# Attention biases gathered on the host, part tiles of queries and keys written in place, and 58 circulating tiles instead of 66

## The chip, the cores and the metric

The kernel runs on one core of a Trainium2 chip. The metric is the time of one execution on the device in microseconds (us), lower is better. The time before is the median of three runs. A profile of one further execution shows where it goes.

The core has five engines with their own instruction queues: TensorE (PE, the matmuls), VectorE (DVE), ScalarE (ACT), GpSimd (POOL) and SyncE (SP, which in this kernel issues all the DMAs). They wait for one another by semaphores alone.

## The reference

Two layers of a diffusion backbone over 256 latent tokens (a grid of 4 rows of 64) and 256 context tokens, 1024 channels. Each layer is a half-step SwiGLU, a mixer of three branches, and a second half-step SwiGLU. Of the mixer only the two attentions matter here. In the last layer only the latent tokens have queries.

```
u = modulate(rmsnorm(h, g_mix[l]), sh2, sc2)
uc = modulate(rmsnorm(hc, g_mix[l]), csh2, csc2)
nq, nk, nv, fu, wq, wk, wv, gl = split_projection(u @ w_in[l])
...
a = neighbourhood_attention(heads(nq, NA_HEADS), heads(nk, NA_HEADS), heads(nv, NA_HEADS),
                            nk_c, nv_c, na_bias[l], rows)
f = fourier_mix(fu)
w = window_gqa_attention(apply_rope(heads(wq, WA_HEADS), cos, sin),
                         apply_rope(heads(wk, WA_KV_HEADS), cos, sin),
                         heads(wv, WA_KV_HEADS), wk_c, wv_c, wa_sink[l])
h = h + gt2 * merge_branches(a, f, w, gl, w_br[l], w_out[l])
```

Inside the neighbourhood attention (8 heads of 64 channels) the scores of the local keys get a bias that depends on the head and on the distance in rows and columns, and keys outside a window of 16 columns are masked:

```
bias = bias_tab[:, dr_idx[:, None, None, :, None], dc_idx[None, :, :, None, :]]
s_loc = jnp.einsum('brcqhd,brcwkhd->bhrcqwk', qg, kb).astype(jnp.float32) * scale + bias[None]
s_loc = jnp.where(in_win[:, :, None, :], s_loc, NEG_INF)
```

The grid has only 4 rows, so every query sees all rows, and the bias of one head is a table of 256 by 256.

## The kernel before

**Precision.** Everything is float32, done on PE as three matmuls of a reduced type: each operand is split into a high part (a copy by ACT) and a low part (the difference, by DVE, or by POOL for weights in some stages). `mm3` (L286 to L291) issues high by high, high by low and low by high.

**Weights** come as 424 tiles of 512 KB in the order of use: SP loads one (L58), ACT writes the high part (L67), DVE or POOL the low part (L76). Loads run five tiles ahead. Between these, DVE works on the sums of the modulation vectors (L311).

**Tiles.** Activations, parts, scores and all temporary tiles (`act` and `tmp`) come from one pool of `N_ACT` = 66 tiles of 128x512 that circulate: a new tile takes the slot that was freed first, and its writer waits for the last reader of the old one, which can be a DMA.

**The mixer** (`mix`) first runs the fourier branch's first part and the values of the neighbourhood attention, then `attention`, a software pipeline written out in steps g. It goes over blocks of two heads: in layer 0 eight neighbourhood and eight windowed blocks (each four for latent and four for context queries), in layer 1 four and four. In a step: the scores of one group on PE (L726, L727), small parts of an earlier block (DVE, L764), transposes (PE, L757) and their high copy (ACT, L759), the weights of the softmax (DVE L733 with the bias as second operand, ACT L735), the values matmuls (PE, L775). At the end of each step `fill` issues projections on PE by the due times in the table `DUES` (names nk, nq for the neighbourhood half, wk, wq for the windowed one), and runs some pieces of the evacuations that wait in `pending`. Nothing reorders instructions: the order of the code is the order on each engine.

**Evacuation of queries and keys.** A projection's PSUM holds two heads, in partitions 0 to 63 and 64 to 127. `plain` (neighbourhood) or `rope` (windowed, after a rotation with four DMAs at L903 and three POOL instructions at L906) makes a high tile (ACT, L889 or L909) and a low tile (DVE, L891 or L911) over all 128 partitions. Then `stack` (L884) moves halves of them by DMA into the tiles that the scores read: for a query two tiles, each of one head's high and low part in the two halves (4 DMAs); for a key four tiles, each with one head's high or low part in both halves (8 DMAs). There are 26 stacks, 13 in each layer. One DMA moves 64 partitions.

**Bias.** The table in memory is a padded one; `na_bias_load` (L707) reads it with a skewed access pattern, 8 DMAs of 64 KB for each pair of heads, in pieces of 64 elements. Four tiles of the pool for each of two buffers hold it. POOL adds the column mask (L711, four instructions for a pair). Eight tiles are cleared by POOL in their context half at the head of each layer (L444).

Of the kernel before, what the change touches and what calls it, by code (L numbers as in the profile page):

```python
# [7 lines left out]
F32 = mybir.dt.float32  # L8
# [19 lines left out]
BIAS_W = 2 * GRID_W - 1  # L28
# [6 lines left out]
N_ACT = 66  # L35
# [224 lines left out]
class Emit:  # L260
# [102 lines left out]
    def setup(self):  # L363
# [56 lines left out]
        self.na_mask = c.tile([128, NLAT], F32, name="na_mask")  # L420
# [5 lines left out]
    def setup_mix(self):  # L426
# [4 lines left out]
        nc.sync.dma_start(out=self.na_mask, in_=d["na_mask"])  # L431
# [262 lines left out]
    def na_bias_load(self, l, p):  # L694


        nc = self.nc
        tab = self.d["na_bias"]
        for i in range(4):
            t4 = self.nab[p % 2][i][:, :NLAT].rearrange("p (r c) -> p r c", c=GRID_W)  # L700
            hp, qt = divmod(i, 2)
            for r2 in range(2):
                first = WIN_R - 1 - (2 * qt + r2)
                off = ((l * 8 + 2 * p + hp) * GRID_W * (2 * WIN_R - 1) + first) * BIAS_W + GRID_W - 1
                src = bass.AP(tensor=tab.tensor, offset=tab.offset + off,
                              ap=[[(2 * WIN_R - 1) * BIAS_W - 1, GRID_W], [BIAS_W, ROWS], [1, GRID_W]])
                nc.sync.dma_start(out=t4[r2 * 64:r2 * 64 + 64], in_=src)  # L707

    def na_bias(self, p):
        for t in self.nab[p % 2]:  # L710
            self.nc.gpsimd.tensor_tensor(out=t[:, :NLAT], in0=t[:, :NLAT], in1=self.na_mask, op=ALU.add)  # L711
# [132 lines left out]
    def mix(self, l, norm, nxt):  # L844
# [9 lines left out]
        self.na_bias(0)  # L854
        self.na_bias_load(l, 1)
# [374 lines left out]
```

## Time and profile before

| what | us |
|---|---|
| median of three runs | 2122.66 |
| lowest and highest run | 2122.08, 2125.06 |
| the profiled execution | 2120.81 |
| span of its profile | 2119.0 |
| PE busy in the span | 2050.9 |
| DVE busy | 1283.7 |
| ACT busy | 848.5 |
| POOL busy | 355.7 |

The span is the time from the first to the last instruction on the core; the rest of the execution's time lies around it. PE's busy time is modelled from the starts of its pipelined matmuls. A row of a timeline gives a start in the span, a duration, the engine, the line of the kernel and the operation with its output and inputs; "x20" says that so many instructions in a row are drawn together, and the bracket at the end gives the idle time of that engine ahead of it and what ended it.

### The profile page before, as it was taken

How to read it: one execution, taken by the hardware profiler on the slowest of the kernel's cores; microseconds unless marked ns; L12 is line 12 of the kernel's file. 1: busy time of each engine (PE TensorE's matmuls, PEld its weight loads, DVE VectorE, ACT ScalarE, POOL GpSimd, SP SyncE). 2: the span in 40 equal slices, each digit the busy share in tenths (PEclk: the TensorE clock that was granted, in tenths of full speed). 3: DMA queues.
4: the chain of work that ended last, by engine and by line, in shares of the span. 5: the costliest groups of instructions: out<-in, count | busy, mean ns of one | idle time of the engine just before them, and what ended most of it. 6: DMA issues, size and time to landing. Idle time of an engine off the chain costs nothing. (4 is left out here: it accounts for less than half of the span.)

```text
span 2119.0 us, 29168 instructions
## 1 busy us (share of the span) xinstructions
PE 2050.9 (97%) x11193; PEld 1764.7 (83%) x11193; DVE 1283.7 (61%) x2035; ACT 848.5 (40%) x1362; POOL 355.7 (17%) x285
## 2 busy tenths in 40 slices
PE   7899999999999999999999989999999989999998
PEld 3688888878888888988888788888888878999998
DVE  6777776566675334687777465533336548566554
ACT  4422222345786222432222243222324458545443
POOL 4200000403441112300000220000012155330002
PEclk9999999999999999999999999999999999999999
DMA  7465566455532333466666545623344563554663
GB/s 271 139 199 182 196 199 212 124 152 144 136 85 73 100 92 98 150 186 193 199 189 200 186 143 186 199 90 100 99 112 145 145 177 110 160 179 153 186 181 109
DMA packets 119412, 327.05 MB, mean 154 GB/s; under 512 B 30692, under 2 KB 35940, under 8 KB 119272
## 3 DMA queue, kind: packets, MB, share of 16 engines
q1 hardware_dynamic: 119272, 325.18, 50.3%
q8 instruction: 88, 1.44, 0.3%
q14 instruction: 52, 0.43, 0.1%
HBM read 305.99 MB, written 1.05 MB: 145 GB/s over the span
## 5 line engine op out<-in xcount | busy, mean ns | idle before, releaser
L290 PE MATMUL ps<-act,wh 128*128 128x512 f32 (+1 forms) x3227 | 1120.9, 347 | 24.1 <-DVE act L229 13.6
L289 PE MATMUL ps<-act,wh 128*128 128x512 f32 (+1 forms) x3227 | 1121.3, 347 | 3.4 <-ACT act L298 1.9
L291 PE MATMUL ps<-act,wl 128*128 128x512 f32 (+1 forms) x3227 | 1118.9, 347 | 1.8 <-DVE wl L76 1.8
L67 ACT ACTIVATE wh<-raw 128x1024 fp32r<-128x1024 f32 x424 | 447.4, 1056 | 707.8 <-PE ps L290 573.7
L290 PEld LDWEIGHTS ps<-act,wh 128*128 128x128 f32 x3227 | 613.2, 190 | 101.8 <-DVE act L229 14.8
L289 PEld LDWEIGHTS ps<-act,wh 128*128 128x128 f32 x3227 | 613.1, 190 | 78.9 <-ACT act L298 2.5
L291 PEld LDWEIGHTS ps<-act,wl 128*128 128x128 f32 x3227 | 613.1, 190 | 77.9 <-DVE wl L76 2.9
L76 DVE TENSOR_TENSOR wl<-raw,wh 128x1024 fp32r<-128x1024 f32 x379 | 474.6, 1254 | 273.6 <-ACT wh L67 273.0
L311 DVE CUSTOM_DVE_ANT_0 dump<-ada,silu_row 128x1024 bf16<-128x1024 f32 x224 | 273.3, 1220 | 13.9 <-DMA ada<-in_w_ada 11.5
L298 ACT ACTIVATE act<-tmp 128x512 fp32r<-128x512 f32 (+1 forms) x122 | 66.9, 566 | 275.2 <-DVE tmp L516 261.8
L471 DVE SCALAR_TENSOR_TENSOR h<-ps,mod,h 128x256 f32<-128x256 f32 x136 | 61.7, 480 | 150.8 <-PE ps L291 150.8
L76 POOL TENSOR_TENSOR wl<-raw,wh 128x1024 fp32r<-128x1024 f32 x45 | 110.7, 2461 | 222.9 <-ACT wh L67 199.7
L454 POOL TENSOR_TENSOR tmp<-h 128x512 f32<-128x512 f32 (+1 forms) x7 | 11.6, 1661 | 782.3 <-DVE h L471 639.8
L516 DVE TENSOR_TENSOR tmp<-tmp,ps 128x512 f32<-128x512 f32 (+1 forms) x88 | 54.6, 621 | 112.1 <-PE ps L291 107.5
L299 DVE TENSOR_TENSOR act<-tmp,act 128x512 fp32r<-128x512 f32 (+1 forms) x122 | 74.3, 625 | 62.2 <-ACT act L298 62.2
L764 DVE TENSOR_TENSOR act<-ps,act 128x512 fp32r<-128x512 f32 x80 | 54.8, 685 | 35.8 <-ACT act L759 27.6
L735 ACT ACTIVATE tmp<-tmp,sm 128x512 f32<-128x512 f32 (+1 forms) x96 | 62.2, 648 | 32.8 <-DVE sm L733 31.5
L775 PE MATMUL ps<-act 128*128 128x256 f32 x320 | 63.0, 309 | 12.4 <-DVE act L764 11.2
L460 POOL TENSOR_TENSOR tmp<-h 128x256 f32<-128x256 f32 (+1 forms) x44 | 51.7, 1174 | 117.8 <-DVE h L471 112.9
L759 ACT ACTIVATE act<-ps 128x512 fp32r<-128x512 f32 x80 | 47.5, 593 | 39.9 <-PE ps L757 34.5
L444 POOL MEMSET tmp<- 128x256 f32 x16 | 4.8, 312 | 348.6 <-PE ps L291 347.9
L775 PEld LDWEIGHTS ps<-act 128*128 128x128 f32 x320 | 44.8, 189 | 17.5 <-DVE act L764 15.0
(110 smaller groups left out, 1372.8 us busy)
## 6 DMA issues: line engine op xcount, KB each, us to landing
raw<-in_ws SPq DMA_DIRECT2D x424, 512.0 KB, 3.7
ada<-in_w_ada SPq DMA_DIRECT2D x128, 512.0 KB, 3.9
act<-act SPq DMA_DIRECT2D x112, 128.0 KB, 2.3
tmp<-in_w_ada_sc SPq DMA_DIRECT2D x16, 256.0 KB, 5.2
tmp<-in_w_ada SPq DMA_DIRECT2D x16, 256.0 KB, 6.0
tmp<-in_na_bias SPq DMA_DIRECT2D x64, 64.0 KB, 2.7
h<-in_h SPq DMA_DIRECT2D x8, 256.0 KB, 5.2
act<-act SPq DMA_DIRECT2D x32, 64.0 KB, 2.0
```

What stands on the lines that cost most here:

```text
L67: self.nc.scalar.activation(out=wh, in_=self.raw[i], func=AF.Copy)
L76: self.lo_engine.tensor_tensor(out=wl, in0=self.raw.pop(i), in1=self.hi[i].bitcast(F32), op=ALU.subtract)
L289: mm(ps, lhsT=w[0], rhs=x[0], start=start, stop=False)
L290: mm(ps, lhsT=w[0], rhs=x[1], start=False, stop=False)
L291: mm(ps, lhsT=w[1], rhs=x[0], start=False, stop=stop)
L298: nc.scalar.activation(out=hi, in_=src, func=AF.Copy)
L299: nc.vector.tensor_tensor(out=lo, in0=src, in1=hi.bitcast(F32), op=ALU.subtract)
L311: self.nc.vector.tensor_tensor_reduce(out=self.dump[:, ks], in0=w, in1=self.silu_row[:, v, ks], scale=1.0, scalar=m if half else 0.0, op0= ...
L471: self.nc.vector.scalar_tensor_tensor(out=h, in0=ps, scalar=self.mod[l, g][:, v, j:j + 1], in1=h, op0=ALU.mult, op1=ALU.add)
L735: nc.scalar.activation(out=e[:, :nk], in_=e[:, :nk], func=AF.Exp, scale=-1.0, bias=nm, accum_out=b["sum"][:, i:i + 1])
L764: nc.vector.tensor_tensor(out=t[1], in0=ps, in1=t[0].bitcast(F32), op=ALU.subtract)
L775: nc.tensor.matmul(b["ps"][hp][:, :256], lhsT=v, rhs=t[j][:, cs], start=c == 0 and j == 0, stop=c == n - 1 and j == 1)
```

## The change

The change has four parts.

1. **Bias.** The host gathers the biases with the mask into a table of one tile of 128x4x256 for each layer and pair of heads. The kernel loads it with one DMA of 512 KB for each pair. Two fixed tiles of 128x4x512 take the place of eight tiles of the pool. Their context halves are cleared once, at the start of the program, by two POOL instructions instead of sixteen in all. Both first pairs are loaded ahead of the layer's mixer, and pair p + 2 after the weights of block p. POOL's additions of the mask and the mask itself are gone.
2. **Stacks.** `stack` now is the evacuation itself. ACT writes the high part of each head straight into its half of the tile (two instructions of 64 partitions), DVE the low part (two of 64 partitions, into the other half of the same tile for a query). A query needs no DMA, a key four, each of which copies one half of a tile into its other half. The intermediate high and low tiles are gone.
3. The pool has 58 tiles.
4. The host's preparation of the two tables follows.

In counts: bias DMAs 64 to 8, part DMAs 144 to 40, ACT and DVE instructions 26 more each, POOL instructions 46 fewer. The rows of PE are the same in number and order.

```diff
-N_ACT = 66
+N_ACT = 58
...
+        self.nab = [c.tile([128, 4, NT], F32, name=f"nab{i}") for i in range(2)]
+        for t in self.nab:
+            nc.gpsimd.memset(t[:, :, NLAT:], 0.0)
...
-        self.nab = [[self.tmp() for _ in range(4)] for _ in range(2)]
-        for t in self.nab[0] + self.nab[1]:
-            self.nc.gpsimd.memset(t[:, NLAT:], 0.0)
         self.na_bias_load(l, 0)
+        self.na_bias_load(l, 1)
...
+        self.nc.sync.dma_start(out=self.nab[p % 2][:, :, :NLAT], in_=self.d["na_bias"][l, p])
...
-        self.na_bias(0)
-        self.na_bias_load(l, 1)
...
-        def stack(name, hi, lo, n):
-
-
-            a, b = self.act(), self.act()
+        def stack(name, src, scale, n):
+
+
             x, y = slice(0, 64), slice(64, 128)
+            a, b = self.act()[:, :n], self.act()[:, :n]
             if "q" in name[0]:
-                moves = (a, x, hi, x), (a, y, lo, x), (b, x, lo, y), (b, y, hi, y)
-                res[name] = a, b
+                parts = (a, x, a, y, x), (b, y, b, x, y)
+                moves = ()
             else:
-                c, d = self.act(), self.act()
-                moves = ((a, x, hi, x), (a, y, hi, x), (b, x, hi, y), (b, y, hi, y),
-                         (c, x, lo, x), (c, y, lo, x), (d, x, lo, y), (d, y, lo, y))
-                res[name] = a, b, c, d
-            for t, i, s, j in moves:
-                nc.sync.dma_start(out=t[i, :n].bitcast(F32), in_=s[j, :n].bitcast(F32))
+                c, d = self.act()[:, :n], self.act()[:, :n]
+                parts = (a, x, c, x, x), (b, y, d, y, y)
+                moves = (a, x, y), (b, y, x), (c, x, y), (d, y, x)
+            for hi, i, _, _, s in parts:
+                nc.scalar.activation(out=hi[i], in_=src[s], func=AF.Copy, scale=scale)
+            yield
+            for hi, i, lo, j, s in parts:
+                nc.vector.scalar_tensor_tensor(out=lo[j], in0=src[s], scalar=scale, in1=hi[i].bitcast(F32),
+                                               op0=ALU.mult, op1=ALU.subtract)
+            for t, i, j in moves:
+                nc.sync.dma_start(out=t[j].bitcast(F32), in_=t[i].bitcast(F32))
+            res[name] = (a, b) if "q" in name[0] else (a, b, c, d)
...
-        def bias_ahead(p):
-            self.na_bias(p)
-            if p < 3:
-                self.na_bias_load(l, p + 1)
...
-                            after=(lambda: bias_ahead(p + 1)) if lat and p < 3 else None,
-                            mask=self.nab[p % 2] if lat else [zero] * 4,
+                            after=(lambda: self.na_bias_load(l, p + 2)) if lat and p < 2 else None,
+                            mask=[self.nab[p % 2][:, i, :] for i in range(4)] if lat else [zero] * 4,
```

Three places show how the order of instructions changes. The first is SP's queue in layer 1's attention, ahead of and behind the first bias load between two blocks; raw is a weight tile, act with 64x512 or 64x256 a part move. Before:

```order
L884 DMA act_13638<-act_13632 64x512 x2
L58 DMA raw_13667<-in_ws 128x1024
L707 DMA tmp_12402<-in_na_bias 64x4x64 x2
L707 DMA tmp_12403<-in_na_bias 64x4x64 x2
L707 DMA tmp_12404<-in_na_bias 64x4x64 x2
L707 DMA tmp_12405<-in_na_bias 64x4x64 x2
L884 DMA act_13697<-act_13693 64x256
L884 DMA act_13697<-act_13694 64x256
L884 DMA act_13698<-act_13694 64x256
L884 DMA act_13698<-act_13693 64x256
L58 DMA raw_13740<-in_ws 128x1024
```

The same place of SP's queue in the changed kernel:

```order
L870 DMA act_13474<-act_13474 64x512
L57 DMA raw_13503<-in_ws 128x1024
L694 DMA nab0_279<-in_na_bias 128x4x256
L57 DMA raw_13561<-in_ws 128x1024
L870 DMA act_13581<-act_13581 64x512
L870 DMA act_13582<-act_13582 64x512
L870 DMA act_13583<-act_13583 64x512
L870 DMA act_13584<-act_13584 64x512
L57 DMA raw_13633<-in_ws 128x1024
```

The eight bias DMAs became one, the query's four moves between two weight loads are gone, and the next key has four moves instead of eight.

The second is DVE's queue at the stack of the windowed keys in layer 1; L733 (ISA) are the weights, L764 the low part that the values matmuls read. Before:

```order
L733 ISA tmp_14090,sm_13962<-ps_14074,tmp_12405 128x512
L733 ISA sm_13962 128x1
L911 SCALAR_TENSOR_TENSOR act_14104<-tmp_13991,act_14103 128x512
L764 TENSOR_TENSOR act_14087<-ps_14081,act_14086 128x512
L733 ISA tmp_14156,sm_14140<-ps_14144,tmp_12406 128x512
```

In the changed kernel (L716 is the former L733, L867 the former L911, L747 the former L764):

```order
L716 ISA tmp_13892,sm_13764<-ps_13876,nab0_279 128x512
L716 ISA sm_13764 128x1
L867 SCALAR_TENSOR_TENSOR act_13903<-tmp_13793,act_13901 64x512
L867 SCALAR_TENSOR_TENSOR act_13904<-tmp_13793,act_13902 64x512
L747 TENSOR_TENSOR act_13889<-ps_13883,act_13888 128x512
L716 ISA tmp_13950,sm_13934<-ps_13938,nab1_280 128x512
```

One instruction of 128 partitions ahead of the low part became two of 64.

The third is POOL's queue at the start of the program; L76 is a weight's low part, L221 and L229 lead to the first projection's operand. Before:

```order
L454 TENSOR_TENSOR tmp_211<-h0_112 128x512
L76 TENSOR_TENSOR wl_261<-raw_136,wh_259 128x1024
L221 TENSOR_TENSOR tmp_287<-h0_112,tmp_268 128x512
L221 TENSOR_TENSOR tmp_301<-h1_113,tmp_268 128x512
L229 TENSOR_TENSOR act_291<-tmp_288,act_290 128x512
```

In the changed kernel:

```order
L452 TENSOR_TENSOR tmp_211<-h0_112 128x512
L75 TENSOR_TENSOR wl_261<-raw_136,wh_259 128x1024
L421 MEMSET nab0_279 128x4x256
L421 MEMSET nab1_280 128x4x256
L220 TENSOR_TENSOR tmp_290<-h0_112,tmp_268 128x512
L220 TENSOR_TENSOR tmp_304<-h1_113,tmp_268 128x512
L228 TENSOR_TENSOR act_294<-tmp_291,act_293 128x512
```

The two memsets came in between the first low part of a weight and the first L221.

## Rows read from the trace of the kernel before

**Rows 1.** The page's first part: busy us of an engine, its share of the span, and its instructions.

```profile
PE 2050.9 (97%) x11193; PEld 1764.7 (83%) x11193; DVE 1283.7 (61%) x2035; ACT 848.5 (40%) x1362; POOL 355.7 (17%) x285
```

**Rows 2.** The windows: from and to in us, length, then the busy time (and instructions) of PE, PE's weight load, DVE, ACT and POOL, the granted clock of PE as a share of full speed, the DMA share and GB/s.

```profile
500.00:640.00 140.00, 135.16 (x758) 114.47 (x757) 98.30 (x254) 102.95 (x256) 63.11 (x53) 1.00 0.48 124
...
1700.00:1750.00 50.00, 40.12 (x256) 35.55 (x255) 23.17 (x52) 27.30 (x56) 29.13 (x26) 0.97 0.65 164
...
1715.00:1720.00 5.00, 1.67 (x8) 1.47 (x9) 2.70 (x6) 1.90 (x4) 1.23 (x2) 0.85 0.90 303
1720.00:1725.00 5.00, 4.59 (x28) 4.00 (x26) 1.12 (x3) 2.63 (x5) 2.40 (x1) 0.81 0.94 202
```

**Rows 3.** The timeline of PE from 1716 to 1724 us.

```profile
1716.16 0.62 PE L775 MATMUL ps<-act 128*128 128x256 f32 x3 [2.86 <-DVE act L764]
1718.95 1.12 PE L932 MATMUL ps<-ident,tmp 128*128 128x128 f32 x4 [2.17 <-ACT tmp L928]
...
1720.08 0.41 PE L290 MATMUL ps<-act,wh 128*128 128x256 f32 x1
1720.29 0.41 PE L291 MATMUL ps<-act,wl 128*128 128x256 f32 x1
...
1723.25 0.28 PE L289 MATMUL ps<-act,wh 128*128 128x256 f32 x1
1723.37 0.28 PE L290 MATMUL ps<-act,wh 128*128 128x256 f32 x1
```

**Rows 4.** The timeline of SP's queue, 1664 to 1752 us; the second number is the time that SP took to issue them.

```profile
1670.34 17.01 SPq L884 DMA_DIRECT2D act<-act  x20
...
1706.67 7.82 SPq L884 DMA_DIRECT2D act<-act  x12
...
1716.14 5.93 SPq L707 DMA_DIRECT2D tmp<-in_na_bias  x8
```

**Rows 5.** The timeline of DVE, 1705 to 1726 us.

```profile
1707.56 0.42 DVE L891 SCALAR_TENSOR_TENSOR act<-ps,act 128x256 fp32r<-128x256 f32 x1 [7.51 <-DMA act<-act]
...
1715.42 0.69 DVE L764 TENSOR_TENSOR act<-ps,act 128x512 fp32r<-128x512 f32 x1 [7.37 <-DMA act<-act]
```

**Rows 6.** The timeline of PE at three other gaps, one in layer 0 and two in layer 1.

```profile
514.53 0.50 PE L726 MATMUL ps<-act 128*128 128x512 f32 x1 [1.83 <-DMA act<-act]
...
1747.27 0.47 PE L726 MATMUL ps<-act 128*128 128x512 f32 x1 [0.41 <-DMA act<-act]
...
1749.70 0.62 PE L775 MATMUL ps<-act 128*128 128x256 f32 x3 [1.18 <-DVE act L764]
```

**Rows 7.** Groups of instructions by line and form: count, busy us in all, mean ns of one, idle time before them and what ended it.

```profile
L889 ACT ACTIVATE act<-ps 128x512 fp32r<-128x512 f32 x12 | 7.0, 584 | 1.4 <-PE ps L291 1.4
L889 ACT ACTIVATE act<-ps 128x256 fp32r<-128x256 f32 x4 | 1.5, 367 | 0.0
L781 ACT ACTIVATE tmp<-ps 64x256 f32<-64x256 f32 x96 | 36.1, 376 | 2.3 <-PE ps L775 1.2
L911 DVE SCALAR_TENSOR_TENSOR act<-tmp,act 128x512 fp32r<-128x512 f32 x6 | 5.0, 831 | 4.1 <-ACT act L909 4.1
L911 DVE SCALAR_TENSOR_TENSOR act<-tmp,act 128x256 fp32r<-128x256 f32 x4 | 3.8, 946 | 6.1 <-ACT act L909 6.1
...
L76 DVE TENSOR_TENSOR wl<-raw,wh 128x1024 fp32r<-128x1024 f32 x379 | 474.6, 1254 | 273.6 <-ACT wh L67 273.0
```

**Rows 8.** Layer 0's windowed blocks: the timeline of DVE and of PE at one stack, and PE's waits for DVE's low part, in all, their number and the longest, first from 480 to 720 us (layer 0), then from 1730 to 1800 us (layer 1).

```profile
590.54 0.69 DVE L911 SCALAR_TENSOR_TENSOR act<-tmp,act 128x512 fp32r<-128x512 f32 x1 [0.65 <-ACT act L909]
...
591.91 0.63 PE L775 MATMUL ps<-act 128*128 128x256 f32 x3 [0.34 <-DVE act L764]
...
PE ps L775 <- DVE act L764: 2.2, 7, 0.3
...
PE ps L775 <- DVE act L764: 6.2, 6, 1.9
```

**Rows 9.** Layer 1's windowed stacks: the timelines of DVE and POOL.

```profile
1733.73 1.22 DVE L911 SCALAR_TENSOR_TENSOR act<-tmp,act 128x512 fp32r<-128x512 f32 x1 [1.41 <-ACT act L909]
...
1746.39 2.38 POOL L76 TENSOR_TENSOR wl<-raw,wh 128x1024 fp32r<-128x1024 f32 x1
...
1746.92 2.13 DVE L911 SCALAR_TENSOR_TENSOR act<-tmp,act 128x256 fp32r<-128x256 f32 x1 [2.02 <-ACT act L909]
...
1773.46 0.46 DVE L911 SCALAR_TENSOR_TENSOR act<-tmp,act 128x256 fp32r<-128x256 f32 x1 [1.38 <-ACT act L909]
```

**Rows 10.** The head of the mixer in layer 0 and in layer 1: timelines of DVE, POOL and PE.

```profile
417.33 0.82 DVE L214 SCALAR_TENSOR_TENSOR act<-tmp,mod,act 128x256 fp32r<-128x256 f32 x1
...
1615.34 3.55 POOL L711 TENSOR_TENSOR tmp<-tmp,na_mask 128x256 f32<-128x256 f32 x4
...
1618.22 2.88 DVE L76 TENSOR_TENSOR wl<-raw,wh 128x1024 fp32r<-128x1024 f32 x2
...
1620.02 0.50 PE L587 MATMUL ps<-wl,act 128*128 128x512 f32 x1 [2.11 <-DVE wl L76]
...
1627.18 0.48 DVE L214 SCALAR_TENSOR_TENSOR act<-tmp,mod,act 128x256 fp32r<-128x256 f32 x1
```

**Rows 11.** POOL's timeline at the start of the program and at the first eight memsets.

```profile
32.25 1.67 POOL L229 TENSOR_TENSOR act<-tmp,act 128x512 fp32r<-128x512 f32 x1 [2.27 <-ACT tmp L227]
...
232.18 2.80 POOL L444 MEMSET tmp<- 128x256 f32 x8 [158.34 <-PE ps L291]
```

More of the change, by code (lines that the diff above doesn't have):

```diff
@@ L27 @@
 WINDOW = 128
-BIAS_W = 2 * GRID_W - 1
 O_NA_Q, O_NA_K, O_NA_V, O_FN, O_WA_Q, O_WA_K, O_WA_V, O_GATE = (
@@ L430, in setup_mix @@
         nc.sync.dma_start(out=self.sin, in_=d["sin"])
-        nc.sync.dma_start(out=self.na_mask, in_=d["na_mask"])
         nc.sync.dma_start(out=self.wa_mask, in_=d["wa_mask"])
@@ L694, in na_bias_load @@
     def na_bias_load(self, l, p):
[L697 to L711, printed above, removed]
+        self.nc.sync.dma_start(out=self.nab[p % 2][:, :, :NLAT], in_=self.d["na_bias"][l, p])
     def attention(self, makers, fill):
@@ L868, in project @@
                 yield
[L870 to L873 removed]
+        def stack(name, src, scale, n):
             x, y = slice(0, 64), slice(64, 128)
+            a, b = self.act()[:, :n], self.act()[:, :n]
             if "q" in name[0]:
[L876 to L894 removed]
+                parts = (a, x, a, y, x), (b, y, b, x, y)
+                moves = ()
+            else:
+                c, d = self.act()[:, :n], self.act()[:, :n]
[10 more added lines that the diff above has]
+            res[name] = (a, b) if "q" in name[0] else (a, b, c, d)
+        def plain(scale):
+            return lambda name, ps, n: stack(name, ps[:, :n], scale, n)
         def rope(scale):
@@ L907, in evac @@
                 yield 1
-                hi, lo = self.act(), self.act()
-                nc.scalar.activation(out=hi[:, :n], in_=t, func=AF.Copy, scale=scale)
-                yield
-                nc.vector.scalar_tensor_tensor(out=lo[:, :n], in0=t, scalar=scale, in1=hi[:, :n].bitcast(F32),
-                                               op0=ALU.mult, op1=ALU.subtract)
-                stack(name, hi, lo, n)
+                yield from stack(name, t, scale, n)
             return evac
@@ L1137, in constants @@
     cos, sin = np.cos(ang).T, np.sin(ang).T
-    c = np.arange(GRID_W)
-    start = np.clip(c - WIN_C // 2, 0, GRID_W - WIN_C)
-    inside = (c[None] >= start[:, None]) & (c[None] < start[:, None] + WIN_C)
-    na = np.where(inside, 0.0, NEG).astype(f)
     band = np.where(np.abs(t[:, None] - t[None]) <= WINDOW, 0.0, NEG).astype(f).reshape(2, 128, NLAT)
@@ L1154, in constants @@
         "sin": np.concatenate([-sin, sin] * 2, 0),
-        "na_mask": np.tile(na, (2, ROWS)),
         "wa_mask": wa,
@@ L1175, in pack @@
     a["w_ada_sc"] = w["w_ada"][0, :, D:2 * D].reshape(KD, 128, 2, 512).transpose(2, 0, 1, 3)
-    pad = GRID_W - WIN_C
-    t = np.pad(w["na_bias"], ((0, 0), (0, 0), (0, 0), (pad, pad)))
-    a["na_bias"] = np.broadcast_to(t[:, :, None], t.shape[:2] + (GRID_W,) + t.shape[2:])
+    c, t = np.arange(GRID_W), np.arange(NLAT)
+    start = np.clip(c - WIN_C // 2, 0, GRID_W - WIN_C)
+    inside = (c[None] >= start[:, None]) & (c[None] < start[:, None] + WIN_C)
+    row, col = t // GRID_W, t % GRID_W
+    dr = row[None] - row[:, None] + WIN_R - 1
+    dc = np.clip(col[None] - col[:, None], 1 - WIN_C, WIN_C - 1) + WIN_C - 1
+    b = np.full((DEPTH, 8, NLAT, NLAT), NEG, np.float32)
+    inside = np.tile(inside, (ROWS, ROWS))
+    b[:, :, inside] = w["na_bias"][:, :, dr[inside], dc[inside]]
+    a["na_bias"] = b.reshape(DEPTH, 4, 2, 2, 128, NLAT).transpose(0, 1, 4, 2, 3, 5).reshape(DEPTH, 4, 128, 4, NLAT)
     s = w["wa_sink"]
@@ L1209 @@
     "c": (128, KD, 2), "b_ada": (128, DEPTH, 9, KD), "gains": (128, DEPTH, 3, 8), "g_final": (128, 8),
-    "na_bias": (DEPTH, 8, GRID_W, 2 * WIN_R - 1, BIAS_W), "sink": (DEPTH, 4, 4), "ident": (128, 128),
-    "cos": (128, NLAT), "sin": (128, NLAT), "na_mask": (128, NLAT), "wa_mask": (128, 2, NT),
+    "na_bias": (DEPTH, 4, 128, 4, NLAT), "sink": (DEPTH, 4, 4), "ident": (128, 128),
+    "cos": (128, NLAT), "sin": (128, NLAT), "wa_mask": (128, 2, NT),
     "dft_n": (128, 2 * NLAT), "dft_d": (128, 256),
```

9 lines of the change are left out of this document (removed).

## The prediction

> **What bounds the kernel now.** I read the busy shares first [rows 1]: TensorE (PE) is busy for 97% of the span. The order of its instructions is the same in both programs, row for row, so the change can win or lose only what PE waits for, some 68 us in all. Next I read the windows [rows 2], to see which stage holds such waits near the edit. Layer 0's attention, 500 to 640 us, has 4.84 us of idle PE in 140. The stretch 1700 to 1750 us, the head of layer 1's attention, has 9.88 in 50, and 3.33 of these fall into 1715 to 1720 alone. Then I read PE's own timeline there [rows 3]: two gaps, 2.86 us ahead of a values matmul that waits for VectorE's (DVE's) low part, and 2.17 us ahead of a transpose that waits for ScalarE (ACT). Why both engines are late stands in the queue of SyncE (SP) [rows 4] and in their own rows [rows 5]. SP issues part moves and bias pieces back to back from 1670 to 1722 us. The low part of a projection waits 7.51 us and the next low part 7.37 us, both released by a part move. An act slot is free only when the moves that read it have gone, and SP issues one in 0.65 to 0.85 us (7.82 us for 12 moves, 17.01 us for 20). So at this place SP's queue, not an engine, sets the end. It is the one place where the removed work is on the path for long.
>
> **The change, part by part.**
>
> *Term A, the queue in layer 1.* Between 1670 and 1722 us SP issues 48 part moves and 16 bias pieces. In the new order the same stretch has 16 part moves (keys only) and two bias loads. At 0.65 to 0.85 us each that is 12 to 15 us of issuing in 52, so the backlog cannot form. Besides, no slot that a query's parts need is held by a DMA any more. I count both gaps as gone: 2.86 + 2.17 = 5.03 us. The clock goes with them: the granted clock is 0.85 and then 0.81 in the two windows after the gap [rows 2], and matmuls of 256 columns start 0.21 us apart there, against 0.12 after 1723 us [rows 3]. Ten of them, and the scores behind, lose 1.2 us. A = **6.2 us**. What is late next there is the usual chain of a block, ACT's copy and DVE's low part, whose gaps are priced below (term E). A new wait is SP's own: the load of the pair two ahead stands right behind the weights of the block that last read that buffer, so SP waits for DVE there, with weight tiles queued behind. Weights are loaded five tiles ahead, so I price that at nothing; if the cover were gone it would be one wait of up to about 1 us for each of 4 loads.
>
> *Term B, later part moves.* The scores at 1747.27 us wait 0.41 us for a move, and the values matmul at 1749.70 another 1.18 us for a low part that came behind a slowed stack [rows 6]. I take the whole of the first and half of the second: **1.0 us**, between 0.4 and 1.6.
>
> *Term C, layer 0.* One scores matmul at 514.53 us waits 1.83 us for a move [rows 6]. It is a query's or a key's; SP's backlog is gone in either case, but a key still has one move per part where it had two. I take **1.8 us** (at worst half of it).
>
> *Term D, POOL's additions of the mask.* 32 of these go. Most run beside nothing that PE waits for. At the head of each mix four of them run beside DVE's evacuations [rows 10]: in layer 1 a pair of weight subtractions takes 2.88 us, where one takes 1.25 on average [rows 7], and PE waits 2.11 us for it; in layer 0 an L214 beside them takes 0.82 us, one that stands alone 0.48. I count 0.7 for layer 1 and 0.5 for layer 0: **1.2 us** (from 0 to 2).
>
> Gains: 6.2 + 1.0 + 1.8 + 1.2 = 10.2 us.
>
> *Term E, the added halves.* Each of 26 stacks has one more ACT and one more DVE instruction, since each now writes 64 partitions. Half the partitions do not halve the time: ACT's copies of 64x256 take 376 ns, those of 128x256 take 367 [rows 7]. So a 512-column stack adds 0.58 us on ACT [rows 7] and 0.69 on DVE [rows 8], a 256-column one 0.37 [rows 7] and 0.46 [rows 9]. The two overlap: DVE can take the first half while ACT writes the second, so the delay of what stands behind is about one half-instruction, start to start: I use 0.62 us for 512 columns (0.69 less the 0.07 by which rows of one engine overlap) and 0.4 for 256. The 16 stacks of the neighbourhood half lie where DVE and ACT wait more than they work (DVE 98 of 140 us in layer 0 [rows 2]), and PE showed no gap behind them but those above: I take nothing, at most 0.62 each. The five windowed ones in layer 0 are different. There DVE's row stands right ahead of the low part that PE waits for: L911 at 590.54, and PE's gap of 0.34 us ends at 591.91 [rows 8]. A gap there means no slack, so the half adds its full 0.6 us. PE has seven such gaps in layer 0's attention, and I take four of the five stacks to have one: 2.4 us. In layer 1, from 1730 us on, there are six, up to 1.9 us long. The first stack has 512 columns, but today it is slowed to 1.22 us beside POOL's mask additions, which go (one alone takes 0.69), so it comes out even [rows 9]; the other four, of 256 columns, add 0.4 us each, 1.6 us (0 to 1.8). E = **4.0 us**, between 1 and 8.
>
> *Term F, the two memsets at the start.* Sixteen memsets leave a place where POOL is idle, and two of 128x4x256 come in ahead of the first L221, on the way to PE's first projection. By elements they cost what eight did, 2.80 us [rows 11]. POOL is idle for 2.27 us before its L229 at 32.25 (it waits for ACT), which covers all but 2.8 - 2.3 = 0.5 us. L221 slows DVE beside it, and that moves along: I take **0.6 us**, between 0 and the whole 2.8 if the cover is gone.
>
> *Term G, 58 slots in place of 66.* Eight slots went to the two bias tiles, which held eight before; the stacks hold two tiles less while they run. Whether PE's reading of an old tile now holds up a new one no row can tell, since before it never came so close. Below it is 0, above the 2.86 us of the gap that such a wait made in [rows 3]; I take **0.5 us**, near the lower end, because a slot returns as soon as its last reader is done, and that is now an engine a few instructions back instead of a queue of DMAs.
>
> Sum: -10.2 + 4.0 + 0.6 + 0.5 = -5.1 us. On the profiled execution, 2120.81 us (its span is 2119.0), this gives 2115.7. That execution lies 1.85 us under the median of the runs, 2122.66, so for the median I say **2117.6 us**.
>
> **A rule of the skill, as a rival.** Two of the windowed stacks' DVE instructions are far longer beside POOL's work: 1.22 us, and 2.13 beside a subtraction of 2.38 us on POOL that began 0.53 us earlier, against 0.46 alone [rows 9]. Over all ten, 8.8 us against about 6.0 at their undisturbed lengths [rows 7]: 2.8 us of excess. Mechanism: each such instruction reads two SBUF tiles, and stands still until POOL's instruction is done; two halves can be caught twice, if POOL gets its next instruction in between them. Price: once more 2.8 us, all of it ahead of low parts that PE waits for, so -5.1 + 2.8 = -2.3, or 2120.4 us. For it: POOL is busy 63.11 of 140 us in layer 0's attention [rows 2], so a next instruction is often ready. Against it: the halves are issued without a gap, and POOL's row is mostly over when the first begins. The Trainium skill states this as a lock (SBUF — State Buffer, "Who interferes with whom"): a VectorE instruction with two SBUF inputs and a GpSimd instruction that reads SBUF block one another, and the one issued second waits for all of the other. The 2.13 us here agrees with a wait nearly as long as the rest of POOL's 2.38; by that rule the sum would be -2.3.
>
> **Other rivals.** *Slower: the halves cost everywhere.* If ACT and DVE have no slack in the neighbourhood stages either, all 26 stacks come through: 18 x 0.62 + 8 x 0.4 = 14.4 us in place of 4.0. Then the sum is -10.2 + 14.4 + 1.1 = +5.3, or 2128 us. It decides for slower once the halves cost over 13.3 us. For it: ACT's copy and DVE's low part stand in the same chain at every stack. Against it: PE showed gaps of 0.34 us at most behind such rows in layer 0. *No gain: the stall comes back.* The gap in layer 1 may come from too many live tiles, with the DMAs only the last reader in the row; with 58 slots the writer then waits for PE's reads at the same place. A falls from 6.2 to about 1.5 us: -0.4, or 2122.3 us. Against it: the 7.5 us waits are released by moves, which are gone. *More gain: the halves hide.* If E is 1 and D 2, the sum is -11.0 + 1.0 + 1.1 = -8.9: 2113.8 us, and with no cost in F and G 2112.7, down to 2111 if B is 1.6 and a gap of about 1 us behind a windowed stack closes as well.
>
> **How the numbers follow.** My forecast, 2115 to 2120, has a chance of 0.50, the larger gain 0.14, the halves caught by POOL 0.13, the stall that returns 0.13, and the halves everywhere 0.10. A measurement of this kernel can tell a change of about 0.2%, 4.25 us, from none: faster is under 2118.4, slower over 2126.9. The forecast's upper end (0.08), the rival by POOL and the returned stall are within it: same 0.34; slower 0.10; faster 0.56. The range leaves out the halves everywhere and the last of the larger gain: 2111 to 2124.
>
> **What would show it.** In the new profile: SP's rows between 1660 and 1720 us with gaps; no DVE or ACT wait on a part move of several us; PE's gaps at the first layer 1 block gone, with a granted clock of 1.00 there; DVE's halves as pairs of about 0.69 us with PE gaps of 0.6 to 1 us behind those of the windowed stacks; the first L221 some 2.8 us later, and PE's first L229 wait at most 0.6 us longer. I am wrong if PE's gap at 1716 stays under another releaser, or if new gaps of 0.3 to 0.6 us appear behind the neighbourhood stacks of layer 0.

## The result, and the profile after

The changed kernel is slower: 2133.93 us (median of four runs, 2131.18 to 2135.33) against 2122.37 for the kernel before, ratio 1.0053 with a 95% interval of 1.0036 to 1.0071. The forecast was 2117.6, its range 2111 to 2124. The profiled execution has a span of 2132.3 us, 13.3 more than before.

The page's first part of the changed kernel answers to [rows 1]:

```profile
PE 2058.4 (97%) x11193; PEld 1770.6 (83%) x11193; DVE 1311.7 (62%) x2061; ACT 864.5 (41%) x1388; POOL 328.3 (15%) x239
```

PE has the same instructions and is busy for 7.5 us more; it is idle for 73.9 us where it was 68.1, 5.8 more. The two make the 13.3. So over half of the net loss is not idle time at all: matmuls ran longer, at a lower clock. The windows of the changed kernel (columns as in [rows 2]) show where:

```profile
500.00:640.00 140.00, 129.59 (x693) 109.19 (x692) 100.02 (x236) 98.80 (x234) 48.43 (x35) 0.96 0.27 77
580.00:585.00 5.00, 3.39 (x12) 2.61 (x13) 3.07 (x10) 2.61 (x7) 0.00 (x0) 0.77 0.02 6
640.00:700.00 60.00, 57.37 (x305) 47.84 (x304) 38.36 (x85) 45.06 (x106) 16.72 (x13) 1.00 0.25 71
1700.00:1750.00 50.00, 44.54 (x270) 38.86 (x268) 32.52 (x61) 30.29 (x61) 25.69 (x18) 0.97 0.52 146
1750.00:1800.00 50.00, 41.55 (x299) 38.73 (x299) 41.22 (x79) 37.38 (x92) 25.10 (x18) 0.93 0.27 80
1785.00:1790.00 5.00, 3.96 (x17) 3.86 (x18) 4.88 (x9) 2.64 (x6) 2.38 (x1) 0.50 0.16 29
```

PE's idle time in layer 0's attention went from 4.84 to 10.41 us [rows 2], although the gap of 1.83 us at its head [rows 6] is gone. The head of layer 1's attention, 1700 to 1750 us, went from 9.88 to 5.46, much as forecast; the next 50 us have 8.45, where they had 3.14. And behind most of the new gaps the granted clock falls: 0.77 from 580 to 585 us, 0.50 (the lower level, 1.2 of 2.4 GHz) from 1785 to 1790. Fewer matmuls fit into such a stretch, and they count as busy.

Fixed stretches of time hold different work in the two kernels. PE's rows are the same in number and order, so the same matmuls can also be found in both traces by their place in the order. Two stretches of the kernel before, layer 0's windowed blocks and layer 1's attention behind its head:

```profile
560.19:640.01 79.82, 76.81 (x443) 64.94 (x442) 61.55 (x161) 65.08 (x170) 34.98 (x30) 1.00 0.38 101
1725.96:1800.08 74.12, 67.49 (x508) 62.64 (x509) 58.98 (x123) 59.67 (x142) 44.38 (x36) 1.00 0.41 116
```

The same matmuls in the changed kernel:

```profile
559.57:654.21 94.64, 82.61 (x442) 68.83 (x441) 70.50 (x166) 68.97 (x175) 34.91 (x30) 0.95 0.20 58
1731.88:1813.97 82.09, 70.94 (x508) 65.85 (x509) 64.58 (x128) 62.28 (x147) 41.93 (x32) 0.94 0.30 86
```

They take 14.8 us longer in layer 0 (9.0 of idle time, 5.8 of longer matmuls) and 8.0 longer in layer 1 (4.5 and 3.5). That is 22.8 us lost. The profiled execution is only 13.3 longer, so all other stretches together gained about 9.5.

PE's timeline in layer 0's windowed blocks has three new gaps:

```profile
581.61 0.62 PE L758 MATMUL ps<-act 128*128 128x256 f32 x3 [2.32 <-DVE act L747]
...
599.06 0.62 PE L758 MATMUL ps<-act 128*128 128x256 f32 x3 [2.54 <-DVE act L747]
...
623.60 1.01 PE L758 MATMUL ps<-act 128*128 128x256 f32 x3 [2.55 <-DVE act L747]
```

The bracket names the low part that the values matmuls read, as in [rows 8], where the gap behind a stack was 0.34. What made it late stands in the timelines of DVE and POOL. First the kernel before, at the same stack:

```profile
576.98 0.69 DVE L911 SCALAR_TENSOR_TENSOR act<-tmp,act 128x512 fp32r<-128x512 f32 x1 [1.18 <-ACT act L909]
...
577.06 2.84 POOL L76 TENSOR_TENSOR wl<-raw,wh 128x1024 fp32r<-128x1024 f32 x1
```

Then the changed kernel:

```profile
576.98 3.44 DVE L867 SCALAR_TENSOR_TENSOR act<-tmp,act 64x512 fp32r<-64x512 f32 x2 [1.19 <-ACT act L864]
...
577.07 2.81 POOL L75 TENSOR_TENSOR wl<-raw,wh 128x1024 fp32r<-128x1024 f32 x1
...
577.70 2.73 DVE L867 SCALAR_TENSOR_TENSOR act<-tmp,act 64x512 fp32r<-64x512 f32 x1
...
580.88 0.67 DVE L747 TENSOR_TENSOR act<-ps,act 128x512 fp32r<-128x512 f32 x1
```

(The row at 577.70 is the second half by itself; the row at 576.98 has both.) Read them together. In both kernels a weight's low part on POOL begins, by its row, some 0.1 us after DVE's instruction. It takes 2.8 us there instead of the usual 2.4, which I read as a wait for DVE. Before, DVE was then done, and its next low part (L764, with an input in PSUM) did not mind POOL. Now a second half is next. It is issued right behind the first, but POOL's instruction stands ahead of it, and the half takes 2.73 us. The pair takes 3.44 us, to 580.42, 0.5 us past POOL's end at 579.88. Undisturbed, the two would have ended at about 578.4. The low part behind them comes some 2 us late, and PE waits. The second half reads nothing that this instruction of POOL writes, and no semaphore is between them. So engines here do not wait for one another by semaphores alone, and such a wait shows in no bracket, only as a longer instruction.

Of the ten pairs three take 3.44 or 3.45 us, all in layer 0. Four take 0.4 to 1.2 us more than undisturbed, beside shorter instructions of POOL or the end of a longer one, and three lose nothing.

### The profile page after: what moved, and what is told of

The parts are those of the page before. It is cut to its first block, busy times and chain, and to the rows that moved or that the text cites. A ratio compares the mean times of both kernels' runs of the same rounds, so it can differ in the third digit from the quotient of the medians.

```text
span 2132.3 us, 28797 instructions
## 1 busy us (share of the span) xinstructions
PE 2058.4 (97%) x11193; PEld 1770.6 (83%) x11193; DVE 1311.7 (62%) x2061; ACT 864.5 (41%) x1388; POOL 328.3 (15%) x239
## 3 DMA queue, kind: packets, MB, share of 16 engines
HBM read 305.86 MB, written 1.05 MB: 144 GB/s over the span
## 5 line engine op out<-in xcount | busy, mean ns | idle before, releaser
L747 DVE TENSOR_TENSOR act<-ps,act 128x512 fp32r<-128x512 f32 x80 | 55.0, 687 | 25.4 <-ACT act L742 24.5
L735 DVE TENSOR_SCALAR tmp<-tmp,sm 128x512 f32<-128x512 f32 (+1 forms) x96 | 59.1, 657 | 1.1
```

The source lines that it names most:

```text
L735: nc.vector.tensor_scalar(out=e, in0=e, scalar1=b["r"][:, i:i + 1], scalar2=None, op0=ALU.mult)
```

## The experiments

Three theories were set against one another. **1:** between two halves on DVE, each with both inputs in SBUF, POOL gets in with an instruction that reads SBUF, and the second half waits for all of it. **2:** 58 tiles are too few. **3:** the halves cost their own length in the chain, as term E of the prediction had it. All ratios are against the kernel before on the same chip.

### Which stacks

**windowed_whole** takes the ten windowed stacks back to the form of before and leaves the rest of the change:

```diff
-                yield from stack(name, t, scale, n)
+                yield from moved(name, t, scale, n)
```

(`moved` is the old evacuation: one ACT and one DVE instruction of 128 partitions, then `stack`'s old moves.) Expected:

> The changed kernel with its ten windowed stacks (wk, wq) made as before: one ACT and one DVE instruction over 128 partitions, then the moves by DMA; the neighbourhood stacks, the bias and the 58 tiles stay as changed. Theory 1 (between the two halves of a windowed low part a POOL instruction gets in, and the second half waits for all of it): the DVE instructions take 0.5 to 1.3 us each again, PE's idle time in layer 0's windowed blocks falls from 9.8 us (560 to 640) to 3 to 4, the clock stays at 1.00, and the time is 2113 to 2119 us. Theory 2 (58 tiles are too few, and writers wait for readers): each of these stacks needs two more tiles, so the gaps stay or grow: 2133 us or more. Theory 3 (the halves cost their own length everywhere, with POOL or without): 16 of 26 stacks still have halves, so two thirds of the loss stay: about 2129 us.

Measured: 2118.23 us, ratio 0.9981 (0.9972 to 0.9989). Some 16 us of the changed kernel's time went with ten pairs of halves, while 16 stacks still had theirs. That fits theory 1 and not 3. In layer 0 the matmuls counted above take the time of the kernel before again (79.96 us against 79.82), at full clock:

```profile
558.32:638.28 79.96, 76.96 (x442) 64.92 (x441) 61.81 (x161) 65.02 (x170) 35.10 (x30) 1.00 0.38 101
```

In layer 1 they still take 5.6 us longer than before; late tiles have a part in that (below).

**neighb_whole** is the mirror image (`plain` calls `moved`, `rope` the new `stack`). Expected:

> The mirror image: the sixteen neighbourhood stacks (nk, nq) as before, whole and with moves by DMA, the windowed ones in halves as changed. Theory 1: the pairs of windowed halves still take up to 3.4 us beside POOL, the gaps of 2 to 4 us stay, and some of the queue of SP in layer 1 comes back: 2133 to 2140 us. Theory 3: ten of 26 stacks have halves left, so the time is about 2126 us.

Measured: 2140.53 us, ratio 1.0083 (1.0070 to 1.0096). That is 0.5 us past what theory 1 expected. The gaps of 2.3 to 2.6 us are all there, and SP's moves cost some more (a scores matmul in layer 0 waits 4.57 us for one, where it waited 1.83 in the kernel before): theory 1 again, and far from theory 3's 2126.

**before_split** asks the question from the other side: the kernel before, with nothing changed but the windowed low part cut in two.

```diff
-                nc.vector.scalar_tensor_tensor(out=lo[:, :n], in0=t, scalar=scale, in1=hi[:, :n].bitcast(F32),
-                                               op0=ALU.mult, op1=ALU.subtract)
+                for s in slice(0, 64), slice(64, 128):
+                    nc.vector.scalar_tensor_tensor(out=lo[s, :n], in0=t[s], scalar=scale, in1=hi[s, :n].bitcast(F32),
+                                                   op0=ALU.mult, op1=ALU.subtract)
```

> The kernel before with one edit: each of its ten windowed low parts is made by two DVE instructions of 64 partitions instead of one of 128; ACT, the moves, the bias and the 66 tiles are as before. Theory 1 (POOL gets in between two halves): the pairs take up to 3.4 us, PE's gaps in layer 0's windowed blocks grow from 0.34 to over 2 us at three or four stacks, the clock falls behind them, and the time is 2128 to 2136 us. Theory 3 (the halves cost their own length): ten times at most 0.6 us, 2122 to 2128 us. If the loss needs ACT's halves or the 58 tiles as well: 2121 to 2124 us.

Measured: 2147.09 us, ratio 1.0111 (1.0096 to 1.0125), 24 us slower, more than expected and twice the loss of the whole change. Ten additional DVE instructions did that. The timelines of DVE and POOL at one stack, and the group by line and form:

```profile
577.67 3.44 DVE L912 SCALAR_TENSOR_TENSOR act<-tmp,act 64x512 fp32r<-64x512 f32 x2 [1.53 <-ACT act L909]
...
577.75 2.81 POOL L76 TENSOR_TENSOR wl<-raw,wh 128x1024 fp32r<-128x1024 f32 x1
```

```profile
L912 DVE SCALAR_TENSOR_TENSOR act<-tmp,act 64x512 fp32r<-64x512 f32 x12 | 15.6, 1302 | 4.6 <-ACT act L909 4.4
```

Neither ACT's halves nor the tiles are needed for the loss. The matmuls counted above take 16.2 and 8.9 us longer here than in the kernel before, 25.1 of the 26.4 us between the two spans:

```profile
560.23:656.29 96.06, 82.83 (x443) 69.48 (x441) 70.61 (x166) 65.42 (x170) 35.22 (x30) 0.93 0.32 84
1743.50:1826.48 82.98, 70.20 (x508) 65.20 (x509) 63.96 (x128) 59.50 (x142) 45.19 (x36) 0.96 0.37 104
```

The changed kernel loses 22.8 us there. That it is slower by only half as much is due to what it gains elsewhere.

### Is it POOL's reading?

**pool_writes_only** leaves DVE as it is in the changed kernel and takes POOL's reads away. It leaves out the low parts of the weights that POOL makes during attention; they are zeros.

```diff
+            if self.lo_engine is self.nc.gpsimd and self.clear:
+                self.raw.pop(i)
+                self.nc.gpsimd.memset(wl.bitcast(F32), 0.0)
```

> The changed kernel with the low parts of the weights that POOL makes during attention left out: POOL clears those tiles instead (an instruction that writes and reads nothing), so the products with these low parts are missing. DVE and ACT have the same instructions as in the changed kernel. Theory 1 (the second half waits while POOL reads SBUF): pairs of windowed halves of 64x512 fall from 3.4 to about 1.3 us, the PE gaps of 2.3 to 2.6 us in layer 0 to under 1 us, and the time to 2117 to 2124 us. Theory 3 (the halves cost their own length): DVE's work is unchanged, so about 2134 us. A third possible reading, that POOL's mere being busy slows DVE, expects pairs of 1.9 us or so beside a clearing instruction of about 1 us.

Measured: 2115.80 us, ratio 0.9972 (0.9961 to 0.9983). The same pair of halves, beside an instruction of POOL that starts at the same point but only writes (timelines, then the group by line and form):

```profile
576.12 1.40 DVE L872 SCALAR_TENSOR_TENSOR act<-tmp,act 64x512 fp32r<-64x512 f32 x2 [1.19 <-ACT act L869]
...
576.19 0.95 POOL L78 MEMSET wl<- 128x1024 f32 x1
```

```profile
L872 DVE SCALAR_TENSOR_TENSOR act<-tmp,act 64x512 fp32r<-64x512 f32 x12 | 8.6, 721 | 4.2 <-ACT act L869 4.0
```

1.40 us for the pair instead of 3.44, and a mean of 721 ns, where the changed kernel's groups by line and form have 1270; its halves that read PSUM, by contrast, are not slowed, though seven of the 32 run beside a subtraction on POOL:

```profile
L867 DVE SCALAR_TENSOR_TENSOR act<-ps,act 64x512 fp32r<-64x512 f32 x24 | 16.5, 688 | 12.0 <-ACT act L864 11.5
L867 DVE SCALAR_TENSOR_TENSOR act<-tmp,act 64x512 fp32r<-64x512 f32 x12 | 15.2, 1270 | 4.2 <-ACT act L864 4.0
```

The clearing instruction is shorter too (0.95 against 2.4 us), so being short could explain a part; but the pair loses almost nothing, not a wait of 0.9 us. The Trainium skill (SBUF — State Buffer, "Who interferes with whom") says exactly this: a VectorE instruction with two SBUF inputs contends with a GpSimd instruction that reads SBUF, not with one that only writes it, and the later one waits for all of the other. The runs agree: 3.44 us beside the instruction that reads, 1.40 beside the one that only writes, 688 ns a half with an input in PSUM.

The time came out 1.2 us below what theory 1 expected. In layer 0 the matmuls counted above take 3.0 us longer than in the kernel before, not 14.8; that is near the 2.4 us that term E has for this layer. In layer 1 3.4 of the 8.0 us stay:

```profile
558.73:641.54 82.81, 77.49 (x443) 65.07 (x441) 60.24 (x166) 68.49 (x175) 22.90 (x30) 1.00 0.24 66
1719.77:1797.29 77.52, 69.18 (x508) 64.90 (x509) 55.57 (x130) 62.07 (x147) 27.03 (x32) 0.96 0.31 92
```

There POOL's rotation, which this run leaves as it is, reads two tiles, and a pair beside it is as long as in the changed kernel, 1.82 us against 1.40 undisturbed (DVE and POOL):

```profile
1727.70 1.82 DVE L872 SCALAR_TENSOR_TENSOR act<-tmp,act 64x512 fp32r<-64x512 f32 x2 [1.40 <-ACT act L869]
...
1727.76 1.21 POOL L891 TENSOR_TENSOR tmp<-tmp,sin 128x256 f32<-128x256 f32 x1
```

**halves_apart** keeps DVE's halves and POOL's reads and puts a step of the pipeline between the halves:

```diff
             for hi, i, lo, j, s in parts:
+                if late and lo is not parts[0][2]:
+                    yield 1
```

> The changed kernel, but the second half of a windowed low part is issued one step of the pipeline later, so that the low part which the values matmuls read stands between the halves. Theory 1: POOL's instruction still gets in behind the first half, but the values' low part (one operand in PSUM) does not wait for it, so a half meets POOL's instruction only if that one is still running: most gaps of 2.3 us shrink to under 1 us, 2118 to 2126 us. Theory 3: the work is the same and stands in the same chain: about 2134 us.

Measured: 2126.35 us, ratio 1.0019 (1.0010 to 1.0027): half of the loss over windowed_whole stays, and the time is 0.35 us past what theory 1 expected. A mean of 1227 ns for its windowed 64x512 halves says that they still meet POOL; but the low part that PE needs no longer stands behind them.

**low_on_pool** gives the windowed low halves to POOL, so that POOL's own order keeps them from its weights (the scale goes into the first copy):

```diff
+                if name[0][0] == "w":
+                    nc.gpsimd.tensor_tensor(out=lo[j], in0=src[s], in1=hi[i].bitcast(F32), op=ALU.subtract)
```

> The changed kernel with the windowed low halves made by POOL instead of DVE (the scale, a power of two, is put into the first copy, so a subtraction is enough). Then POOL's own order keeps a weight's low part and a half apart, and DVE's instruction ahead of the values' low part is gone. Theory 1: the gaps of 2 to 4 us behind windowed stacks go, 2113 to 2121 us; POOL has some 26 us more to do, and if it becomes late with the weights' low parts PE shows gaps that wait for them. Theory 3: half of the added work, ACT's, stays in the chain: 2122 to 2128 us.

Measured: 2118.53 us, ratio 0.9985 (0.9977 to 0.9994). ACT's halves are still there, DVE's are gone, and the time is that of windowed_whole. PE has no gap of 2 us left in the two attentions, and no lower clock. But it is so in the sum only: in layer 0 the matmuls counted above still take 7.7 us longer than before, in layer 1 none. What POOL's own time for the halves and ACT's halves have in the 7.7 us was not tried.

### The tiles and the bias

**halves_62_tiles** is the changed kernel with 62 tiles. Room for four more comes from keeping the zeros of the context half once in each bias tile:

```diff
-N_ACT = 58
+N_ACT = 62
-        self.nab = [c.tile([128, 4, NT], F32, name=f"nab{i}") for i in range(2)]
+        self.nab = [c.tile([128, 5, NLAT], F32, name=f"nab{i}") for i in range(2)]
...
-                            mask=[self.nab[p % 2][:, i, :] for i in range(4)] if lat else [zero] * 4,
+                            mask=[self.nab[p % 2][:, i::4 - i, :][:, :2] for i in range(4)] if lat else [zero] * 4,
```

> The changed kernel with 62 circulating tiles: the zeros of the bias tiles' context halves are kept once in each bias tile and read by a stepped pattern, which frees the room. Theory 1: DVE's and ACT's waits in the windowed blocks are not for slots, so 2131 to 2136 us. Theory 2 (58 tiles are too few): the waits behind the halves go too, under 2126 us.

Measured: 2134.85 us, ratio 1.0053 (1.0040 to 1.0066), the changed kernel's own. Theory 2 falls for the change as it stands.

It does not fall for the others. **windowed_whole_62**:

> The kernel with whole windowed stacks, and 62 tiles in the same way. With 58 its trace has DVE's low parts in layer 1 released by POOL's rotation (1.42 and 2.40 us) and one DVE instruction by a part move (1.51 us), though neither is an operand of them: slots that come back late. If that is so, these waits go and PE's gaps in layer 1's windowed blocks shrink by 3 to 5 us: 2113 to 2116 us. If the slots are not the cause: 2117 to 2119 us as with 58.

Measured: 2114.95 us, ratio 0.9962 (0.9950 to 0.9975), 3.3 us under the same with 58. The two intervals just touch, so this size is rough. What went are waits like these of windowed_whole, on DVE's and POOL's timelines:

```profile
1728.16 0.69 DVE L747 TENSOR_TENSOR act<-ps,act 128x512 fp32r<-128x512 f32 x1 [1.42 <-POOL tmp L905]
...
1727.41 0.72 POOL L905 TENSOR_TENSOR tmp<-tmp 128x256 f32<-128x256 f32 x1
```

L747 has no operand of POOL's; it waits until POOL has read the tile that was in its slot before (1727.41 + 0.72 = 1728.13).

**bias_only** is the bias part alone, with all stacks as before and 58 tiles, **bias_only_62** the same with 62.

Expected of the first:

> The bias part and the 58 tiles alone: gathered on the host, one load for a pair, no additions on POOL; all 26 stacks whole with moves by DMA as before. Theory 1: no halves, so the windowed gaps are those of before or less; the queue of SP in layer 1 loses 16 of 64 issues and keeps the 48 moves, so the gap of 5 us there shrinks by about a quarter to a half: 2117 to 2122 us. Theory 2: the stacks need their two more tiles from 58: slower than before, 2126 us or more.

and of the second:

> The bias part alone (all 26 stacks whole, with moves by DMA) with 62 tiles instead of the 58 at which it was 3 us slower than before. If slots that come back late were the cause of that: 2117 to 2121 us. If SP's queue, which still has 48 moves to issue in layer 1, is: 2124 to 2127 us, with the gaps at 515 us and at the first block of layer 1 still there.

Measured: 2125.51 us, ratio 1.0011 (1.0002 to 1.0020), and 2114.91 us, ratio 0.9956 (0.9942 to 0.9970). The first lies between what the two theories expected; the second is below both of its ranges. The two profiled executions lie further apart than the medians (2127.18 and 2111.03 us), so their rows overstate the difference. At the place of term A, bias_only's DVE still waits for a part move, if for less than in [rows 5], and this row has no answer in bias_only_62, whose 1700 to 1750 us have 6.76 us of idle PE at full clock. First DVE's timeline of bias_only, then the window of bias_only_62:

```profile
1705.76 0.42 DVE L877 SCALAR_TENSOR_TENSOR act<-ps,act 128x256 fp32r<-128x256 f32 x1 [4.88 <-DMA act<-act]
```

```profile
1700.00:1750.00 50.00, 43.24 (x311) 39.30 (x310) 29.70 (x63) 32.89 (x73) 25.68 (x21) 1.00 0.56 158
```

SP issues the same 48 moves there in both. So taking the 16 bias pieces from SP's queue and giving the pool enough tiles is sufficient for the gap of term A; whether enough tiles alone would do was not tried. And bias_only_62 equals windowed_whole_62 within their scatter: with 62 tiles, the neighbourhood stacks written in place bring no time beyond that of the bias part. They do close one gap: PE's wait of 1.83 us for a move [rows 6] is 1.80 in bias_only_62 and gone in windowed_whole_62.

### A version that beats both

**mixed_62** takes for each layer the windowed form with the smaller idle time of PE: whole in layer 0, low halves on POOL in layer 1.

```diff
+                yield from (moved if l == 0 else stack)(name, t, 1.0, n)
```

> 62 tiles, neighbourhood stacks in halves, the windowed stacks of layer 0 whole with moves, those of layer 1 in halves with the low halves on POOL: for each layer the form whose PE idle time was the smaller one (layer 0, 560 to 700 us: 3.5 against 9.2 us; layer 1, 1700 to 1800 us: 8.6 against 11.4). The two are far apart in the program, so the gains should add: 2111 to 2114 us, against 2115 for the whole form in both layers.

Measured: 2109.63 us, ratio 0.9935 (0.9921 to 0.9950), the fastest of all, below the range that was expected; 24 us below the changed kernel. Its windows have no slow clock and little idle time left:

```profile
560.00:640.00 80.00, 76.95 (x446) 64.93 (x445) 64.10 (x166) 66.89 (x174) 33.20 (x30) 1.00 0.37 100
...
1700.00:1750.00 50.00, 47.06 (x341) 43.05 (x340) 35.97 (x70) 39.27 (x88) 36.59 (x29) 1.00 0.41 119
1750.00:1800.00 50.00, 45.03 (x339) 41.37 (x339) 37.41 (x70) 37.70 (x92) 30.05 (x21) 1.00 0.34 98
```

## Why the prediction was wrong, point by point

**The step that failed is term E's price of the windowed halves**: "A gap there means no slack, so the half adds its full 0.6 us", 4.0 us in all. The place was right, the price was not. It took the second half for a further instruction of known length. It is one more instruction that can be locked out, and in the three worst pairs POOL's next instruction has queued up behind the first half. Such a pair costs 2.0 us of POOL's 2.4 here (up to 2.7 in before_split), and then mostly the clock. In the two stretches counted above the halves stand against a loss of 22.8 us, where the price was 4.0; without POOL's weight reads 3.0 and 3.4 us of it are left.

**The rival "a rule of the skill" was the right one and had 0.13.** It named this mechanism and priced it from the mean excess of instructions that stand alone, 2.8 us for all ten. That price fails for the reason that makes the mechanism: alone, an instruction of DVE often starts first and loses nothing (0.69 us at 576.98 us, with POOL's behind it). The argument against was that "the halves are issued without a gap, and POOL's row is mostly over when the first begins". The first is so and does not help: the second half is issued at 577.70, right behind the first, but POOL's instruction has stood there since 577.07. The second is not so in the three worst pairs: POOL's row begins after the first half. The rows that could have told it were in the trace before: POOL's subtractions right behind a windowed low part take 2.84, 2.85 and 2.88 us at three stacks of layer 0, where 2.4 is usual. POOL waits there at the very point where a second half would start, and these are the three stacks whose pairs take 3.4 us.

**The clock** was counted on the side of the gains only (1.2 us in term A). Net of that gain, longer matmuls made 7.5 of the 13.3 us.

**Term A** held in part. Of its two gaps, 2.86 and 2.17 us [rows 3], the first is gone; PE's next row there still waits 1.39 us for ACT, so 3.6 of 5.0 us came. The granted clock is 1.00 from 1710 to 1740 us, and the matmuls behind the gaps, which the kernel before starts from 1715 to 1725 us, run 1.5 us shorter, where 1.2 were forecast: 5.1 of 6.2 us in all. SP's queue has gaps, as foreseen:

```profile
1700.11 2.56 SPq L870 DMA_DIRECT2D act<-act  x4
1702.76 0.54 SPq L57 DMA_DIRECT2D raw<-in_ws  x1
1705.69 0.60 SPq L694 DMA_DIRECT2D nab<-in_na_bias  x1
1706.38 0.57 SPq L57 DMA_DIRECT2D raw<-in_ws  x1
1712.14 2.56 SPq L870 DMA_DIRECT2D act<-act  x4
```

The cause was told too simply: the bias part and enough tiles do it with all the moves in place.

**Terms B, C, D and F.** B: the wait of 0.41 us for a move is gone, and that of 1.18 behind it is 0.54, 1.05 us against the forecast 1.0. C: no gap at 514 us is left; from 500 to 560 us PE's idle time fell by 1.25 us, where 1.8 were forecast. D: the idle time of 400 to 450 and 1600 to 1650 us fell by 0.45 and 0.71 us, 1.2 as forecast. F: the memsets cost less than by elements, and PE's first wait behind them became shorter, 1.62 us instead of 2.23, so nothing of the 0.6 is seen. PE in the kernel before, then POOL and PE in the changed one:

```profile
33.97 0.50 PE L290 MATMUL ps<-act,wh 128*128 128x512 f32 x1 [2.23 <-POOL act L229]
```

```profile
26.81 1.85 POOL L421 MEMSET nab<- 128x1024 f32 x2
...
33.65 0.50 PE L289 MATMUL ps<-act,wh 128*128 128x512 f32 x1 [1.62 <-POOL act L228]
```

**Term E's nothing for the sixteen neighbourhood stacks** held: one of their two inputs is in PSUM, and their halves are as long as whole instructions (688 ns) without a gap of PE behind them in layer 0.

**Term G** was 0 for the change itself (halves_62_tiles). For whole stacks it was worth 3.3 us with the neighbourhood halves and 10.6 without. So the written-in-place stacks do save tiles. Term C's gap is the other thing that they save.

What stays open: in layer 1 the loss of 8.0 us was not taken apart. POOL's weight reads, its rotation, late tiles and the halves' own length all have a part in it. And the change's own gains, about 9.5 us where 10.2 were forecast, are the rest of a count in one execution of each kernel, which scatters by a few us.

## What to carry to other kernels

Before you cut a VectorE instruction in two, look at what GpSimd has waiting: if the VectorE instruction has two inputs in SBUF and GpSimd's reads SBUF, the cut can let GpSimd in, and the second part then waits for GpSimd's instruction on top of its own length, 2.0 us more here. In a trace, a GpSimd instruction that is some tenths of a us too long right behind a VectorE one is the sign that it stands in line there. And when a pool of tiles shrinks together with the work that used it, run other sizes too: here 58 against 62 tiles hid some 10 us of gain from the bias part.

## What the runs showed of the hardware that was not expected

Not only the halves were caught. In the changed kernel's layer 1 the two scalings of a softmax, each with one tile as input and a column of factors, take 3.60 us beside a POOL subtraction, where such a pair took 0.87 to 1.92 us in the kernel before; the longest gap of PE in that layer, 4.10 us, follows them; that one led to the other is read from the order of the rows, not tried. DVE, POOL and PE:

```profile
1778.75 3.60 DVE L735 TENSOR_SCALAR tmp<-tmp,sm 128x512 f32<-128x512 f32 x2
...
1779.49 2.58 POOL L75 TENSOR_TENSOR wl<-raw,wh 128x1024 fp32r<-128x1024 f32 x1
...
1786.04 1.01 PE L758 MATMUL ps<-act 128*128 128x256 f32 x3 [4.10 <-DVE act L747]
```

A memset on POOL of 128x1024 took some 0.93 us (1.85 for two), one of 128x256 0.35 (2.80 for eight in [rows 11]): its time does not grow in step with the elements. And in the 5 us after five of the changed kernel's new gaps, 2.2 to 4.1 us long, PE's granted clock was between 0.51 and 0.66 (all or part of the time at the lower level), so that they cost clearly more than their own length. But the gap's length does not tell it: after the gap of 2.34 us that ends at 1771.51 the clock stayed at 1.00, and so it did after one of 2.54 us in windowed_whole, as long as one that was followed by 0.66. Two stretches of the changed kernel, behind its gaps of 2.54 and 2.34 us:

```profile
599.06:604.06 5.00, 5.00 (x17) 4.14 (x18) 1.96 (x8) 3.75 (x12) 0.74 (x1) 0.66 0.25 93
1771.51:1776.51 5.00, 5.00 (x39) 4.82 (x40) 4.71 (x11) 3.82 (x9) 1.46 (x1) 1.00 0.26 94
```

PE in windowed_whole, and the 5 us behind that gap:

```profile
1760.31 0.62 PE L758 MATMUL ps<-act 128*128 128x256 f32 x3 [2.54 <-DVE act L747]
...
1760.31:1765.31 5.00, 5.00 (x39) 4.83 (x40) 4.74 (x11) 3.72 (x9) 1.56 (x1) 1.00 0.57 159
```
